# The samples' coefficients of a gated DeltaNet layer, computed beside the prompt's last recurrence, in a pool of their own

## The chip, the cores and the metric

One core of a Trainium2 chip runs the kernel, once per measurement. The metric is the time of one execution in device microseconds (us). Matrix products run on TensorE (PE in the profile; its weight loads are PEld), elementwise work on VectorE (DVE), ScalarE (ACT) and GpSimd (POOL). Every transfer between the chip's main memory and SBUF is issued on SyncE's queue (SP) and carried by 16 DMA engines.

## The reference

The reference is one inference step of a two-layer decoder trunk (model width 1024): a prompt of 1024 tokens, and eight samples of four tokens each that continue from stored caches and states. Layer 0 is sliding-window attention, layer 1 is gated DeltaNet with 16 value heads of width 128 and 8 key heads. Only layer 1 matters here. For each head it carries a state S (128 x 128):

```
S_t = e^{g_t} S_{t-1} + k_t u_t^T
u_t = beta_t (v_t - (e^{g_t} S_{t-1})^T k_t),    o_t = S_t^T q_t / sqrt(dk)
```

For the prompt this is done in chunks along the sequence, starting from zero. For a sample it is done for four tokens, starting from a stored state: 8 samples x 16 heads x 64 KB = 8.4 MB of states are read, and as much is written back as new states. The four steps are not run one by one over the states. With the products of the *old* state with all k and q, the four u and o follow from small coefficients between the four tokens, and the new state is the old one times a decay, plus the sum of k u^T. The output o is normalized, multiplied with a gate, and projected back to width 1024 (w_out, 2048 x 1024); the result is added to the residual, and a final norm gives y.

## The kernel before, in words

The kernel is one program for one core. Its last fifth, where the change lies, consists of an output projection with several smaller jobs woven into it.

**The order of the instructions** is settled when the program is built. Each engine runs its instructions in the order in which the builder recorded them (class `Core`, line 96, keeps modelled free times of the engines; line 89 is the line that all recorded instructions carry in the profile). A job is a Python generator. `weave` (line 483) puts it into a list, sorted by its rank in the table `K` (line 239); `stages` (line 494) is called between matmuls and lets each job advance whose next condition holds in the model: `ready` (operands written), `idle` (engine free), `soon`, `bank` (a PSUM bank of that name is free), `over` (the named jobs have ended). DMA issues on SP are placed by the surrounding scheduler. So the order of the engines reflects modelled times; on the chip an engine that meets an instruction whose operands are late waits, with everything behind it.

**The output projection** (`out_block`, line 2253) runs 18 blocks: 8 of 128 prompt rows and one of the 32 sample rows, first with weight rows 0 to 1023 (part 0), then with rows 1024 to 2047 (part 1). The block of the samples is number 8, and the last but one again in part 1. A prompt block takes 48 matmuls of 128x512 (three products of high and low halves, 8 row tiles, 2 column halves), a sample block 32, together 832. Each block needs two tiles `of` of gated rows (256 KB each, `prepare`, line 2136), a residual tile `xt` (512 KB, `rows_of`, line 2169), and stores 512 KB (`x2d` in part 0, the output y in part 1; `finish`, line 2183). At the samples' block the program opens larger buffers for the states (`wide`, line 2618), and `prepare` for it waits for the job "core" (line 2141).

**The jobs beside it**, in the order in which they depend on each other:

- "chain", "output", "gating" (lines 1935 to 2050): the prompt's last recurrence, eight chunks, each a sequence of TensorE, VectorE and ScalarE steps. It runs during the first blocks of the projection, which then uses the PSUM banks "pj" only.
- "states" (`states_times`, line 2312): reads all 8.4 MB of old states in pieces of 256 KB (four buffers) and multiplies them with the samples' k and q; the products end in `kqs`.
- "core" (line 2365): starts when the recurrence is over. Its **first half** (lines 2388 to 2469) needs no states: it loads the samples' q and k (`qk2`), v (`vs`), the decays (`gH`) and beta (`bH`) from a scratch tensor in main memory, transposes k to the update operand `K96` and q, k, v to a layout with one row per head and sample (`VH`, `QK0`, `QK1`), and computes norms, decays and the coefficients between the four tokens (`cK`, `cQ`, through the work tile `prd`). Its **second half** (from line 2470) waits for "states", transposes their products (`KQT`, `KQ`), computes the four u in place in `VH`, transposes them to the second update operand `U96` (line 2515), tells the job "new" to begin (`updates`, line 2516), and computes the samples' outputs into `gsT`.
- "load" (`second_half`, line 2547): loads and splits the second half of w_out (`whB`, `wlB`).
- "new" (`new_states`, line 2562): the stream of the new states. A piece of four heads (256 KB, pool `su`, three buffers, tile `S1`, shown as `S` in the profile) or, once `wide` is open, of eight heads (512 KB) is loaded; per two heads there is one matmul of `kb` (K96 masked for one sample) with `U96` into a bank of "mi" (two banks), and VectorE adds it to the decayed state; the piece is stored to `out_new_s_s`.

The tiles of "core" lie in a pool `sl` on the right side of SBUF, opened after the recurrence's pools are closed (lines 2368 to 2374); `K96`, `U96` and `gsT` lie on the left in `sp2`, then `kqs`, then the pool `sg` of "states".

Of the kernel before, what the change touches and what calls it, by code (L numbers as in the profile page):

```python
# [5 lines left out]
F32 = mybir.dt.float32  # L6
# [8 lines left out]
P = 128  # L15
# [5 lines left out]
DS = 4  # L21
# [7 lines left out]
HV = 16  # L29
# [188 lines left out]
def body(tc, I, O, cst_ap, dbg=None):  # L218
# [17 lines left out]
    ZB, VB, SB = 1, 3, 4  # L236
    SP = (2, 20)
    AM = (4, 8)
    K = dict(split=3, add=3, attend=12, turning=14, modulate=31, cached=9, wo=7, turn=0, ahead=6, taps=4, gating=5, decay=2, samples=28, load=5, mod=9, shape=9, decays=8, prepare=1, gather=11, finish=54, states=21, core=4, new=9)
    KR = [{'chain': 8, 'output': 9, 'solve': 5, 'invert': 21, 'blocks': 10, 'decayed': 0}, {'chain': 0, 'output': 3, 'solve': 12, 'invert': 10, 'blocks': 35, 'decayed': 35}, {'chain': 33, 'output': 2, 'solve': 22, 'invert': 19, 'blocks': 33, 'decayed': 34}, {'chain': 22, 'output': 12, 'solve': 3, 'invert': 4, 'blocks': 30, 'decayed': 17}, {'chain': 14, 'output': 0, 'solve': 1, 'invert': 17, 'blocks': 31, 'decayed': 57}, {'chain': 3, 'output': 13, 'solve': 6, 'invert': 20, 'blocks': 55, 'decayed': 29}, {'chain': 8, 'output': 1, 'solve': 11, 'invert': 20, 'blocks': 73, 'decayed': 34}, {'chain': 10, 'output': 8, 'solve': 4, 'invert': 28, 'blocks': 40, 'decayed': 44}]  # L240
    TB = (3, 6)
    SW = (1, 16)
# [240 lines left out]
    def weave(gen, name, hq=None):  # L483

        rank = KR[hq][name] if hq is not None else K[name]
        i = 0
        while i < len(jobs) and jobs[i][3] <= rank:
            i += 1
        jobs.insert(i, [lambda: True, gen, name, rank])

    def over(*names):
        return lambda: not any(e[2] in names for e in jobs)
# [25 lines left out]
    def ready(*ts):  # L518
        return lambda: plain() or nc.ready(ts) <= nc.free["tensor"]

    def soon(*ts):
        return lambda: plain() or nc.ready(ts) <= nc.free["tensor"] + AH
# [10 lines left out]
    def bank(tag):  # L533

        q = held.setdefault(tag, [])
        yield lambda: len(q) < banks[tag] or q[-banks[tag]] is None
        t = psb(tag)
        q.append(t.tensor.name)
        yield lambda: plain() or nc.after(nc.used, t, "tensor") <= nc.free["tensor"]
        return t  # L540

    def give(tag, t):
        q = held[tag]
        q[q.index(t.tensor.name)] = None
# [1058 lines left out]
    if True:  # L1603
# [694 lines left out]
        def flat(t_):  # L2298
            return t_.rearrange("p t d -> p (t d)")
# [2 lines left out]
        sp2 = es.enter_context(tc.tile_pool(name="sp2", bufs=1, side="left"))  # L2302

        K96 = sp2.tile([96, HQ * P], F32R, name="K96")
        U96 = sp2.tile([96, HV * P], F32R, name="U96")
        gsT = sp2.tile([P, HV, TS], F32, name="gsT")
        kq_guard = tc.tile_pool(name="kq", bufs=1, side="left")
        kqs = kq_guard.__enter__().tile([P, 2, 512], F32, name="kqs")
        sg_guard = tc.tile_pool(name="sg", bufs=1, side="left")
        sg = Watched(nc, sg_guard.__enter__())  # L2310

        def states_times():
            zq = sg.tile([P, DB, HQ, 32], F32, name="zq")
            qk = sg.tile([P, 4, P], F32, tag="S0", name="qk", bufs=SB).rearrange(
                "p a (c t) -> p (a c) t", t=TS).rearrange("p (i h) t -> p h i t", i=2)
            nc.sync.dma_start(qk.rearrange("p h i t -> p i h t"), smd[0:2 * HQ].rearrange("(i h) p t -> p i h t", i=2))
            us_ = [(g * 4 + b, hd, jj) for g in range(2) for hd in range(2) for b in range(4) for jj in range(2)]
            sts = []

            def fetch():  # L2320
                if len(sts) < len(us_):
                    b, hd, jj = us_[len(sts)]
                    st = sg.tile([P, 4, P], F32, tag="S0", name="S0", bufs=SB)
                    nc.sync.dma_start(st, S0[b][:, 8 * hd + 4 * jj:8 * hd + 4 * jj + 4])
                    sts.append(st)

            for b in range(DB):
                yield idle("gpsimd")
                nc.gpsimd.memset(zq[:, b], 0.0)
            for b in range(DB):  # L2330
                c0 = 8 * (b % 4)
                yield idle("vector", qk)
                nc.vector.tensor_copy(zq[:, b, :, c0:c0 + 8].rearrange("p h (i t) -> p h i t", i=2),
                                      qk[:, :, :, b * DS:(b + 1) * DS])
            for _ in range(SB):
                fetch()
            for u in range(0, len(us_), 2):
                b, hd, _ = us_[u]
                if u % 16 == 0:
                    pk = yield from bank("lg")  # L2340
                yield lambda: pos[0] >= SW[0] + SW[1] * (u + 1) / 10
                yield ready(sts[u], sts[u + 1], zq)
                for j in range(4):
                    nc.tensor.matmul(pk[32 * j:32 * j + 32, hd * 256:(hd + 1) * 256], zq[:, b, 4 * hd + j, :],
                                     sts[u + j // 2][:, 2 * (j % 2):2 * (j % 2) + 2, :].rearrange("p h d -> p (h d)"),
                                     start=(b % 4 == 0), stop=(b % 4 == 3), skip_group_check=True)
                fetch()
                fetch()
                if u % 16 == 14:
                    yield soon(pk)  # L2350
                    nc.scalar.copy(kqs[:, b // 4, :], pk)
                    give("lg", pk)
# [9 lines left out]

    updates, fng, gate_s, sl_guard, su_guard, wo2_guard = [], None, None, None, None, None

    def core():
        nonlocal sm, out_banks, sl_guard
        yield over("chain", "output", "gating")
        g_guard.__exit__(None, None, None)
        sm_guard.__exit__(None, None, None)
        gk_guard.__exit__(None, None, None)  # L2370
        sm = Watched(nc, sm_first, 2)
        out_banks = ("pj", "pj", "tr", "ob")
        sl_guard = tc.tile_pool(name="sl", bufs=1, side="right")
        sl = Watched(nc, sl_guard.__enter__(), since=nc.free["tensor"] + SL)

        def t2(nm, dt=F32):
            return sl.tile([P, DS, P], dt, tag="t2", name=nm, bufs=4)

        def turned(dst, srcs, parts=P):

            yield ready(*srcs)
            pt = yield from bank("lg")
            for q, src in enumerate(srcs):
                nc.tensor.transpose(pt[0:parts, q * P:(q + 1) * P], src, ident)
            yield soon(pt)
            dst(pt)
            give("lg", pt)

        qk = flat(t2("qk2")).rearrange("p (i h t) -> p i h t", i=2, h=HQ)
        nc.sync.dma_start(qk.rearrange("p i h t -> p (i h) t"), smd[0:2 * HQ].rearrange("n p t -> p n t"))  # L2390
        vs = t2("vs")
# [23 lines left out]
                nc.vector.tensor_copy(qv[:, t], src[:, t].unsqueeze(2).to_broadcast([P, HQ, 2, DB]))  # L2415
            QKH.append((yield from by_head(f"QK{i}", [qd[:, t, :] for t in range(DS)])))
        QH, KH = QKH

        def s4(nm, n=DS):
            return sl.tile([P, n], F32, name=nm)  # L2420

        yield idle("vector", gH)
        gcH = s4("gcH")
# [27 lines left out]
        for t in range(DS):  # L2451
            n = t + 1
            dc = s4(f"dc{t}")
            yield idle("vector")
            nc.vector.tensor_tensor(dc[:, 0:n], gcH[:, t:t + 1].to_broadcast([P, n]), gcH[:, 0:n], ALU.subtract)
            nc.scalar.activation(dc[:, 0:n], dc[:, 0:n], AF.Exp)
            yield idle("vector", dc)
            nc.vector.tensor_tensor(dc[:, 0:n], dc[:, 0:n], rkH[:, 0:n], ALU.mult)
            for dst, src in ((cQ, QH), (cK, KH)):
                m = n if dst is cQ else t  # L2460
                if m == 0:
                    continue
                yield idle("vector")
                nc.vector.tensor_tensor(pr_[:, 0:m], KH[:, 0:m], src[:, t:t + 1, :].to_broadcast([P, m, P]), ALU.mult)
                yield idle("vector")
                nc.vector.tensor_reduce(dst[:, t, 0:m], pr_[:, 0:m], AX.X, ALU.add)
                nc.vector.tensor_tensor(dst[:, t, 0:m], dst[:, t, 0:m], dc[:, 0:m], ALU.mult)
            if t > 0:
                nc.vector.tensor_scalar(cK[:, t, 0:t], cK[:, t, 0:t], rkH[:, t:t + 1], -1.0, ALU.mult, ALU.mult)
        yield over("states")  # L2470
        KQT = sl.tile([P, HV * DB, 2, DS], F32, name="KQT")
        kqv = KQT.rearrange("p (a j r g b) i t -> p g a r j (b i t)", a=2, j=4, r=2, g=2)
# [133 lines left out]
            nc.sync.dma_start(S1[b][:, h0:h0 + n], st)  # L2606

    weave(states_times(), "states")
    weave(core(), "core")
    weave(second_half(), "load")  # L2610
    weave(new_states(), "new")
# [9 lines left out]
    su_guard.__exit__(None, None, None)  # L2621
    sl_guard.__exit__(None, None, None)
    wo2_guard.__exit__(None, None, None)
    kq_guard.__exit__(None, None, None)
    ps_guard.__exit__(None, None, None)
    es.close()
# [30 lines left out]
```

## Time and profile before

| what | value |
|---|---|
| median of three runs | 1781.42 us (1780.93 to 1783.7) |
| execution that was profiled | 1771.52 us |
| span of its trace | 1769.7 us |
| granted TensorE clock, mean over the span | 0.984 |
| TensorE busy | 1671.2 us (94%) |
| last projection matmul of the trace begins | 1757.38 us |
| first and last store of a new state | issued at 1637.84 and 1754.43 us |

The profile is of one execution. Its page gives the busy time of each engine, and answers to questions about its trace give busy times by stretch, the waits by engine, and the instructions in order of time with the idle time of the engine before each and what ended it. Names stand for tiles ("ps_mi" is a PSUM tile of the banks "mi"). Overlapping matmuls each show their own latency; the distance between their starts is what they cost.

### The profile page before, as it was taken

Reading aid. Unit: us, or ns where it says so; the run is one execution under the profiler, and the core shown is the slowest. Engines: PE = TensorE matmul, PEld = TensorE weight load, DVE = VectorE, ACT = ScalarE, POOL = GpSimd, SP = SyncE. Lnnn points to the kernel's source line nnn. Section 1 sums busy time; section 2 is a strip of 40 time slices with the busy share of each in tenths; the row PEclk is TensorE's granted clock in tenths of the full one; section 3 lists DMA queues with packets and bytes.
Section 4 is the critical chain, followed back from the end, with each engine's and each line's share of the span. In section 5 each row is a group of like instructions: output and inputs, shape, how many; then the busy total and the mean of one; then the engine's idle time right before and its main releaser. Section 6 shows DMA issues by size and latency. Waiting matters only on the chain. (4 is left out here: it accounts for less than half of the span.)

```text
span 1769.7 us, 32005 instructions
## 1 busy us (share of the span) xinstructions
PE 1671.2 (94%) x10665; PEld 1452.1 (82%) x10665; DVE 1217.1 (69%) x3536; ACT 860.4 (49%) x2513; POOL 625.8 (35%) x1264
## 2 busy tenths in 40 slices
PE   6999999998998698989999999999999998998897
PEld 5978888877776698879989999899999997766685
DVE  4526676554565577886888779788787795458687
ACT  4625565453334446446554564654655664433332
POOL 2501111122112146343453545454445455323322
PEclk9999999999999799999999999999999999999999
DMA  9442122233332231231322323224133127774886
GB/s 325 134 119 59 50 63 54 67 105 101 102 113 89 69 86 47 72 101 35 112 69 58 103 57 105 64 61 119 42 100 84 46 75 205 212 208 129 256 255 184
DMA packets 282582, 191.78 MB, mean 108 GB/s; under 512 B 99369, under 2 KB 254889, under 8 KB 282386
## 3 DMA queue, kind: packets, MB, share of 16 engines
q1 hardware_dynamic: 282418, 189.75, 36.9%
q8 instruction: 84, 1.38, 0.3%
q14 instruction: 80, 0.66, 0.1%
HBM read 144.68 MB, written 47.04 MB: 108 GB/s over the span
## 5 line engine op out<-in xcount | busy, mean ns | idle before, releaser
L89 PE MATMUL ps_pj<-h2hi,wh 128*128 128x384 f32 (+1 forms) x1140 | 387.3, 340 | 2.6 <-ACT wh L89 2.6
L89 PE MATMUL ps_pj<-h2lo,wh 128*128 128x384 f32 (+1 forms) x1140 | 389.1, 341 | 0.0
L89 PE MATMUL ps_pj<-h2hi,wl 128*128 128x384 f32 (+1 forms) x1140 | 384.6, 337 | 1.2 <-POOL wl L89 1.2
L89 POOL TENSOR_TENSOR wl<-wr,wh 128x512 fp32r<-128x512 f32 x123 | 165.4, 1347 | 540.5 <-ACT wh L89 482.1
L89 PEld LDWEIGHTS ps_pj<-h2hi,wh 128*128 128x128 f32 x1140 | 217.2, 190 | 6.5 <-ACT wh L89 3.1
L89 PEld LDWEIGHTS ps_pj<-h2hi,wl 128*128 128x128 f32 x1140 | 217.2, 191 | 5.8 <-POOL wl L89 2.6
L89 PEld LDWEIGHTS ps_pj<-h2lo,wh 128*128 128x128 f32 x1140 | 217.0, 190 | 4.4
L89 POOL TENSOR_TENSOR xt<-xt,y 128x512 f32<-128x512 f32 (+1 forms) x48 | 65.2, 1361 | 196.3 <-DVE y L89 175.3
L89 DVE SCALAR_TENSOR_TENSOR vT<-XR,cT,vT 128x384 f32<-128x384 f32 (+1 forms) x144 | 92.6, 649 | 41.8 <-ACT vT L89 39.7
L89 PE MATMUL ps_pj<-hlo,wh 128*128 128x384 f32 (+1 forms) x360 | 119.3, 332 | 0.0
L89 PE MATMUL ps_pj<-hhi,wh 128*128 128x384 f32 (+1 forms) x360 | 118.6, 330 | 0.0
L89 PE MATMUL ps_pj<-hhi,wl 128*128 128x384 f32 (+1 forms) x360 | 117.9, 328 | 0.0
L89 DVE TENSOR_TENSOR tmp<-X 64x31 f32<-64x31 f32 (+15 forms) x248 | 96.1, 387 | 8.0 <-POOL X L89 4.3
L89 DVE TENSOR_TENSOR X<-X,tmp 64x31 f32<-64x31 f32 (+15 forms) x248 | 92.8, 374 | 8.5
L89 ACT CAST wh<-wr 128x512 fp32r<-128x512 f32 x123 | 75.4, 615 | 17.0 <-PE ps_pj L89 14.5
L89 PEld LDWEIGHTS ps_pj<-hlo,wh 128*128 128x128 f32 x360 | 67.7, 188 | 13.6 <-issue 13.5
L89 POOL TENSOR_TENSOR Xd<-Xc,cst 32x128 f32<-32x128 f32 x128 | 68.5, 535 | 14.8 <-DMA Xc<-Xdd 7.5
L89 PEld LDWEIGHTS ps_pj<-hhi,wh 128*128 128x128 f32 x360 | 67.6, 188 | 5.9 <-issue 4.2
L89 PEld LDWEIGHTS ps_pj<-hhi,wl 128*128 128x128 f32 x360 | 67.7, 188 | 3.3 <-issue 3.3
L89 ACT ACTIVATE qe<-ps_mi,Eg 128x128 f32<-128x128 f32 x112 | 35.0, 363 | 67.6 <-PE ps_mi L89 67.6
L89 ACT ACTIVATE prob<-prob,nm 128x256 f32<-128x256 f32 (+1 forms) x128 | 62.3, 489 | 11.3 <-DVE nm L89 11.1
L89 ACT COPY XR<-ps_pj 128x384 f32<-128x384 f32 (+1 forms) x96 | 43.1, 449 | 47.1 <-PE ps_pj L89 46.4
(564 smaller groups left out, 4281.2 us busy)
## 6 DMA issues: line engine op xcount, KB each, us to landing
wr<-in_gdn_w_in SPq DMA_DIRECT2D x96, 256.0 KB
S<-in_state_gdn_s SPq DMA_DIRECT2D x40, 256.0 KB
xt<-in_x_prompt SPq DMA_DIRECT2D x16, 512.0 KB
wm<-in_w_mod SPq DMA_DIRECT2D x16, 512.0 KB
wr<-in_swa_w_in SPq DMA_DIRECT2D x64, 128.0 KB
wm<-in_w_mod SPq DMA_DIRECT2D x32, 256.0 KB
wmod<-in_w_mod SPq DMA_DIRECT2D x32, 256.0 KB
DP<-gcr SPq DMA_DIRECT2D x64, 128.0 KB
```

What stands on the lines that cost most here:

```text
L89: inst = fn(*args, **kwargs)
```

## The change

The first half of "core" becomes a job of its own, "early", with rank 22 (behind "states" with 21). It no longer waits for the recurrence. Its tiles come from a new pool `sla` on the left side, opened before `sg`, so that it doesn't need the memory which the recurrence's pools hold; the tiles of the four steps that rotate under the tag "t2" come from it too. `U96` moves from `sp2` to the pool `sl` on the right. "core" waits for the recurrence and for "early", takes over its results and goes on with its second half. All other ranks stay. The number of instructions on TensorE is the same, and so is the arithmetic.

```diff
-    K = dict(..., states=21, core=4, new=9)
+    K = dict(..., states=21, early=22, core=4, new=9)
...
-        U96 = sp2.tile([96, HV * P], F32R, name="U96")
+        U96 = None
...
+        sla_guard = tc.tile_pool(name="sla", bufs=1, side="left")
+        sla = Watched(nc, sla_guard.__enter__(), since=nc.free["tensor"])
         sg_guard = tc.tile_pool(name="sg", bufs=1, side="left")
...
+    def t2(nm, dt=F32):
+        return sla.tile([P, DS, P], dt, tag="t2", name=nm, bufs=4)
...
+    early_ = {}
+
+    def core_early():
+
+        sl = sla
         qk = flat(t2("qk2")).rearrange("p (i h t) -> p i h t", i=2, h=HQ)
         nc.sync.dma_start(qk.rearrange("p i h t -> p (i h) t"), smd[0:2 * HQ].rearrange("n p t -> p n t"))
         vs = t2("vs")
...
                 nc.vector.tensor_scalar(cK[:, t, 0:t], cK[:, t, 0:t], rkH[:, t:t + 1], -1.0, ALU.mult, ALU.mult)
+        early_.update(VH=VH, gcH=gcH, bH=bH, at=at_, kd=kdH, eg=egH, rq=rqH, cK=cK, cQ=cQ, pr=pr_)
+
+    def core():
+        nonlocal sm, out_banks, sl_guard, U96
+        yield over("chain", "output", "gating")
+        yield over("early")
+        VH, gcH, bH, at_, kdH, egH, rqH, cK, cQ, pr_ = (early_[n] for n in ("VH", "gcH", "bH", "at", "kd", "eg", "rq", "cK", "cQ", "pr"))
+        g_guard.__exit__(None, None, None)
...
+        U96 = sl.tile([96, HV * P], F32R, name="U96")
         yield over("states")
...
     weave(states_times(), "states")
+    weave(core_early(), "early")
     weave(core(), "core")
```

More of the change, by code (lines that the diff above doesn't have):

```diff
@@ L238, in body @@
     AM = (4, 8)
-    K = dict(split=3, add=3, attend=12, turning=14, modulate=31, cached=9, wo=7, turn=0, ahead=6, taps=4, gating=5, decay=2, samples=28, load=5, mod=9, shape=9, decays=8, prepare=1, gather=11, finish=54, states=21, core=4, new=9)
+    K = dict(split=3, add=3, attend=12, turning=14, modulate=31, cached=9, wo=7, turn=0, ahead=6, taps=4, gating=5, decay=2, samples=28, load=5, mod=9, shape=9, decays=8, prepare=1, gather=11, finish=54, states=21, early=22, core=4, new=9)
     KR = [{'chain': 8, 'output': 9, 'solve': 5, 'invert': 21, 'blocks': 10, 'decayed': 0}, {'chain': 0, 'output': 3, 'solve': 12, 'invert': 10, 'blocks': 35, 'decayed': 35}, {'chain': 33, 'output': 2, 'solve': 22, 'invert': 19, 'blocks': 33, 'decayed': 34}, {'chain': 22, 'output': 12, 'solve': 3, 'invert': 4, 'blocks': 30, 'decayed': 17}, {'chain': 14, 'output': 0, 'solve': 1, 'invert': 17, 'blocks': 31, 'decayed': 57}, {'chain': 3, 'output': 13, 'solve': 6, 'invert': 20, 'blocks': 55, 'decayed': 29}, {'chain': 8, 'output': 1, 'solve': 11, 'invert': 20, 'blocks': 73, 'decayed': 34}, {'chain': 10, 'output': 8, 'solve': 4, 'invert': 28, 'blocks': 40, 'decayed': 44}]
@@ L2363, in body, with s4, turned @@
     updates, fng, gate_s, sl_guard, su_guard, wo2_guard = [], None, None, None, None, None
[L2365 to L2387, printed above, removed]
+    def t2(nm, dt=F32):
+        return sla.tile([P, DS, P], dt, tag="t2", name=nm, bufs=4)
+    def s4(nm, n=DS):
+        return sla.tile([P, n], F32, name=nm)
+    def turned(dst, srcs, parts=P):
+        yield ready(*srcs)
+        pt = yield from bank("lg")
+        for q, src in enumerate(srcs):
+            nc.tensor.transpose(pt[0:parts, q * P:(q + 1) * P], src, ident)
+        yield soon(pt)
+        dst(pt)
+        give("lg", pt)
+    early_ = {}
+    def core_early():
+        sl = sla
         qk = flat(t2("qk2")).rearrange("p (i h t) -> p i h t", i=2, h=HQ)
@@ L2417, in core @@
         QH, KH = QKH
-        def s4(nm, n=DS):
-            return sl.tile([P, n], F32, name=nm)
         yield idle("vector", gH)
@@ L2469, in core @@
                 nc.vector.tensor_scalar(cK[:, t, 0:t], cK[:, t, 0:t], rkH[:, t:t + 1], -1.0, ALU.mult, ALU.mult)
+        early_.update(VH=VH, gcH=gcH, bH=bH, at=at_, kd=kdH, eg=egH, rq=rqH, cK=cK, cQ=cQ, pr=pr_)
[5 more added lines that the diff above has]
+        g_guard.__exit__(None, None, None)
+        sm_guard.__exit__(None, None, None)
+        gk_guard.__exit__(None, None, None)
+        sm = Watched(nc, sm_first, 2)
+        out_banks = ("pj", "pj", "tr", "ob")
+        sl_guard = tc.tile_pool(name="sl", bufs=1, side="right")
+        sl = Watched(nc, sl_guard.__enter__(), since=nc.free["tensor"] + SL)
+        U96 = sl.tile([96, HV * P], F32R, name="U96")
         yield over("states")
@@ L2623, in body @@
     wo2_guard.__exit__(None, None, None)
+    sla_guard.__exit__(None, None, None)
     kq_guard.__exit__(None, None, None)
```

## The prediction

> **What bounds the kernel now.** I read the page's head, then the busy times of five engines by stretch from the end of the last projection on, then what TensorE (PE) waited for there. In a stretch's row the last three numbers are the granted TensorE clock, the DMA engines' share and GB/s.
>
> ```profile
> span 1769.7 us, 32005 instructions
> PE 1671.2 (94%) x10665; PEld 1452.1 (82%) x10665; DVE 1217.1 (69%) x3536; ACT 860.4 (49%) x2513; POOL 625.8 (35%) x1264
> ```
>
> ```profile
> 1494.00:1560.00 66.00, 63.05 (x367) 45.94 (x367) 27.10 (x82) 24.39 (x81) 20.98 (x58) 0.97 0.78 225
> 1560.00:1637.00 77.00, 67.56 (x323) 49.64 (x322) 56.72 (x148) 27.58 (x54) 25.55 (x18) 1.00 0.51 157
> 1637.00:1660.00 23.00, 17.63 (x79) 12.32 (x78) 15.83 (x33) 8.58 (x18) 9.81 (x8) 0.99 0.82 255
> 1660.00:1740.00 80.00, 79.97 (x361) 64.95 (x361) 59.47 (x204) 24.41 (x58) 24.68 (x19) 0.98 0.86 256
> ```
>
> ```profile
> PE ps_mi L89 <- DVE S L89: 4.8, 1, 4.8
> PE ps_mi L89 <- ACT uo L89: 3.1, 2, 2.2
> PE ps_lg L89 <- DVE KQT L89: 3.1, 1, 3.1
> PE ps_mi L89 <- ACT kb L89: 2.1, 2, 1.3
> PE ps_tr L89 <- POOL olo L89: 1.8, 1, 1.8
> ...
> PE ps_lg L89 <- DVE qd L89: 0.9, 1, 0.9
> PE ps_lg L89 <- DMA qk<-smd: 0.8, 1, 0.8
> ```
>
> TensorE sets the end. From 1660 to 1740 us it is busy 79.97 of 80 us. In the 77 us before the sample states start to stream it is idle 9.4, and in the 23 us in which they start, 5.4. It runs its instructions in an order that was written down when the program was built, so a wait is lost for good. The change adds no arithmetic and removes none: it can win idle time only, and it loses each wait that it makes. That caps the gain: the two idle stretches hold 14.8 us.
>
> Next, what TensorE needs for one instruction of the output projection (128x512) and for one state update (ps_mi<-U,kb), and how the stream of the states began.
>
> ```profile
> 1583.16 0.39 PE L89 MATMUL ps_pj<-h2hi,ohi 128*128 128x512 f32 x1
> ...
> 1589.73 0.39 PE L89 MATMUL ps_pj<-h2lo,ohi 128*128 128x512 f32 x1
> ```
>
> ```profile
> 1752.64 0.28 PE L89 MATMUL ps_mi<-U,kb 96*128 96x256 f32 x1
> 1752.75 0.39 PE L89 MATMUL ps_tr<-h2hi,ohi 128*128 128x512 f32 x1
> ```
>
> ```profile
> 1634.07 0.28 PE L89 MATMUL ps_mi<-U,kb 96*128 96x256 f32 x1
> ...
> 1659.82 0.55 PE L89 MATMUL ps_mi<-U,kb 96*128 96x256 f32 x1 [4.85 <-DVE S L89]
> ...
> 1665.47 0.28 PE L89 MATMUL ps_mi<-U,kb 96*128 96x256 f32 x1
> ```
>
> The first pair is 29 steps apart: 6.57 / 29 = 0.2265 us per projection instruction; there are 832 of them, and I use their running number as a place in the program. The second pair gives 0.11 us per update instruction. The third shows the first eight pieces of the states (256 KB each): from the last update of piece 1 (number 372) to that of piece 8 (number 466) lie 94 projection instructions and 14 updates, 94 x 0.2265 + 14 x 0.11 = 22.8 us of work, and 31.4 us passed. **8.6 us were lost while the states came in small pieces.** Afterwards, with pieces of 512 KB, nothing was lost. This is the stretch that the change makes longer.
>
> **The change part by part.** *What moves.* The built programs' order (no times in it) shows that the block from the loads of the samples' q, k, v to the coefficients cK now stands beside the last recurrence. In the trace of before it ran here:
>
> ```profile
> 1572.69 0.85 DVE L89 COPY qd<-qk 128x128 f32<-128x128 f32 x4
> ...
> 1602.23 0.23 DVE L89 TENSOR_SCALAR cK<-cK,rkq 128x3 f32<-128x3 f32 x1
> ```
>
> The last input of the updates, U, is written at number 324 in the program of before and at number 224 in the new one: 100 x 0.2265 = 22.7 us earlier. The first piece leaves at number 287 instead of 372. From number 462 on the buffers of 512 KB are open in the new program (466 before), since that hangs on block 8 of the projection. So **18 pieces of 256 KB and 7 of 512 KB** take the place of 8 and 12, and the states end at number 658 instead of 811.
>
> *What it wins.* The waits for qd, qk, KQT and olo (0.9 + 0.8 + 3.1 + 1.8 = 6.6 us) come from VectorE working through the moved block while TensorE needs copies that stand behind it; with VectorE free there, I let 5.5 us go and keep 1.1 for what is late next (TensorE still needs KQT through a copy on ScalarE and one on VectorE). The second wait for kb (1.3 us of the 2.1) sits at number 765, where no updates are left: it goes as well. Gain: 6.8 us. The 4.8 us for S I do not count as won, because its kind returns below.
>
> *What the small pieces cost.* Two bounds apply to 18 of them. First the work: from number 287 to 462 lie 175 x 0.2265 + 34 x 0.11 = 43.4 us of TensorE. Second the traffic. Counting the built program's DMA issues from behind the first small store to the last: 17 stores and 15 loads of 256 KB, 2 loads of 512 KB, 5 tiles of gated rows (of), 9 moves of 512 KB of the residual (xt, x2d; two of them are the samples' 128 KB), 3 weight pieces and the final gain: 16.5 MB. TensorE at full speed would ask for 16.5 / 43.4 us = 380 GB/s. The same count from small store 1 to 8 in the program of before gives 7.86 MB, and these are their issues:
>
> ```profile
> 1637.84 1.38 SPq L89 DMA_DIRECT2D out_new_s_s<-S  x2
> ...
> 1666.43 0.38 SPq L89 DMA_DIRECT2D out_new_s_s<-S  x1
> ```
>
> 7.86 MB in 28.6 us is 275 GB/s by the stores, in 31.4 us 250 by the updates, where the work alone (22.8 us) asked for 345; the 80 us after it ran at 256 with a share of 0.86. I take 265 GB/s: 16.5 MB then need 62.3 us, and 62.3 - 43.4 = 18.9 us are lost instead of 8.6, so **10.3 us more**. The wait passes from a piece's load to VectorE, which updates in order, from there to the two PSUM banks of the updates, and so to TensorE. With 250 GB/s it is 14.0 more, with 275 8.0. The ends: the fastest and slowest 4 us with a DMA share of 1.09,
>
> ```profile
> 1552.00:1556.00 4.00, 3.64 (x17) 2.67 (x15) 1.17 (x2) 0.00 (x0) 1.28 (x1) 1.00 1.09 238
> 1564.00:1568.00 4.00, 3.87 (x26) 2.03 (x23) 0.00 (x0) 0.00 (x0) 0.16 (x1) 1.00 1.09 361
> ```
>
> give 361 GB/s (45.7 us, 6.3 less than before) and 238 (69.3 us, 17.3 more). The Trainium skill, "DMA: Bandwidth & Descriptors", Specifications, gives a ceiling of about 358 GB/s of HBM per core; by it (an estimate) the 16.5 MB take 46 us, next to nothing is lost, and the change wins. That is the first rival. The row at 361 agrees with that figure as a peak of 4 us; no longer stretch here comes near it.
>
> *The large pieces.* From the last small store to the last large one the new program moves 12.3 MB in 196 x 0.2265 + 28 x 0.11 = 47.5 us, 259 GB/s; 256 was carried without loss. Cost 0, at most 2.
>
> *The start.* Four loads come up from here to the front of the SP queue, behind the projection's first residual tiles:
>
> ```profile
> 1551.36 0.37 SPq L89 DMA_DIRECT2D qk<-smd  x1
> 1551.78 3.15 SPq L89 DMA_DIRECT2D vs<-smd  x1
> 1554.98 1.13 SPq L89 DMA_DIRECT2D gH<-gbr  x1
> 1556.15 0.43 SPq L89 DMA_DIRECT2D bH<-gbr  x1
> ```
>
> That is 5.1 us of SP. Queued behind: two weight pieces (ScalarE splits them for the projection), two tiles of gated rows, the first states. TensorE needs the second half of the gated rows from number 24 on, 24 x 0.2265 = 5.4 us into the projection; the cover is nearly whole. In TensorE's own order the transposes of k stand right after the gate rows, so TensorE waits if they have not landed, and VectorE's step of the recurrence stands behind their copies. Between 0 and 4 us; I take 1. TensorE waits at that place before, too, for the recurrence's uo, so part of it is not new.
>
> *Beside the recurrence.* 20 transposes, their copies, at most the 29.8 us of VectorE between the two rows above, and a table load on ScalarE fall into 1494 to 1560 us, where VectorE is busy 27.1 of 66 and ScalarE 24.4. TensorE has the projection to fill with, as its 63.05 of 66 show. Between 0 and 3; I take 1. What U's move to the pool on the right costs: nothing, its memory is free before U is written.
>
> **Sum.** -5.5 - 1.3 + 10.3 + 0 + 1 + 1 = **+5.5 us** on the span of 1769.7 (1775.2). The execution with the profile took 1771.52 us, the median of the runs shown is 1781.42, 0.56% more; I carry the difference over: 1781.4 + 5.5 = **1786.9 us**. Differences under 0.2% (3.6 us) a measurement of this kernel can hardly tell from none.
>
> One thing can add to a long wait:
>
> ```profile
> 1656.00:1660.00 4.00, 0.18 (x1) 0.21 (x2) 1.28 (x4) 1.43 (x3) 1.26 (x1) 0.96 0.72 229
> 1660.00:1664.00 4.00, 4.00 (x13) 3.24 (x14) 1.78 (x6) 0.61 (x2) 1.27 (x1) 0.61 0.93 263
> ```
>
> After the wait of 4.85 us the granted clock is 0.61 for 4 us: some 1.5 us more. It is within the 31.4 us above, and so in the rate. The Trainium skill, "TensorE: Matmul & The Clock Gate", The HAM clock gate, says the same: half the clock after an idle window of about 3.4 us. By it many short waits cost only themselves.
>
> **The rivals.**
> *A: the DMA engines have room, and the change wins.* Place: the small pieces. It decides at the rate at which the loss there is 8.6 + 4.8 = 13.4 us: 16.5 MB in 56.8 us, 290 GB/s. At 330 (50.0 us, 6.6 lost) the sum is -5.5 - 1.3 - 2.0 + 2 = -6.8: 1774.6 us. For it: the peak of 361, and the DMA share of 0.82 in the first 23 us. Against: three buffers of 256 KB must be loaded, updated, stored and loaded again, and every stretch over 20 us lies at 225 to 256.
> *B: both cancel,* at 280 to 300 GB/s: 1781.4.
> *C: the start decides.* If the samples' k or the weights behind them land 4 us late and the recurrence is held as well, 4 + 3 instead of 2 are added: 1791.9. For it: the transpose of k that stands right behind the gate rows in TensorE's order. Against: the load goes out in the place of one that landed in time.
> *D: the block does not run earlier* since some wait of it stands with the old end: 1781.4. The built order speaks against it (224 for 324).
>
> **How the numbers follow.** Forecast (small pieces at 240 to 280 GB/s): 0.46. A 0.28, B 0.15, C 0.09, D 0.02. Slower by over 0.2%: 0.46 + 0.09 = 0.55; within: 0.17; faster: 0.28. The forecast's own range is 1783 to 1794. The bounds of the unknown costs reach from -5.5 - 1.3 - 6.3 = -13.1 (1768) to -6.8 + 17.3 + 2 + 4 + 3 = +19.5 (1801). Leaving out a tenth at each end: **1770 to 1797**, which takes in A and C.
>
> **What would show it.** Right: the first store of a sample state about 23 us earlier (85 x 0.2265 = 19.3, and 3.5 of waits gone), no wait for KQT or qd, an idle TensorE of some 19 us between the first and the last small store at about 265 GB/s with waits for S and kb, none after. Wrong: TensorE full in that stretch at over 290 GB/s (A), or idle before 1510 us (C).

## The result, and the profile after the change

| | kernel before | changed kernel |
|---|---|---|
| median of 20 runs each | 1780.9 us (1774.97 to 1790.59) | 1785.44 us (1780.55 to 1791.58) |
| execution with the profile | 1771.52 us | 1784.83 us |

**The change makes the kernel slower: ratio 1.003, 95% interval 1.0017 to 1.0043.** The medians are 4.5 us apart. In a second comparison (run "again", below) the medians are 7.5 us apart and the ratio was 1.0041, 1.0026 to 1.0056. The forecast was +5.5 us. The two profiled executions are 13.3 us apart, more than that: the one of before is 9.4 us under the median of the 20 runs (it is not one of them, and it is quicker than the quickest, 1774.97), the one of after 0.6 under. So sizes are taken from the ratios first, and from traces where several of them agree.

The page of the changed kernel begins:

```profile
span 1783.0 us, 32028 instructions
PE 1678.2 (94%) x10665; PEld 1453.6 (82%) x10665; DVE 1215.4 (68%) x3536; ACT 861.4 (48%) x2513; POOL 629.5 (35%) x1264
```

On TensorE the two programs have the same order up to the transposes of k that stand in front of the projection. I set the clock to zero at a TensorE instruction ahead of it (the eight ps_lg<-UZ,M of 128x96, at 1485.15 us before and 1489.14 after: 4.0 of the 13.3 us have passed by then) and cut the rest at the projection's instructions number 40, 159, 287 and 462 (counted from 0; the last is number 831). Busy times by stretch, the kernel before and then the changed one; first the stretch and its length, then PE, PEld, DVE, ACT and POOL, at the end granted clock, DMA share and GB/s:

```profile
1485.15:1517.09 31.94, 28.10 (x146) 20.12 (x147) 15.79 (x51) 13.73 (x41) 10.59 (x31) 0.89 0.82 238
1517.09:1565.02 47.93, 46.34 (x278) 32.52 (x274) 15.81 (x41) 15.03 (x47) 17.20 (x39) 1.00 0.82 233
1565.02:1607.84 42.82, 37.06 (x175) 27.50 (x173) 34.21 (x88) 16.59 (x34) 14.91 (x10) 1.00 0.56 177
1607.84:1664.55 56.71, 48.47 (x217) 36.24 (x216) 40.68 (x99) 19.67 (x38) 19.44 (x14) 0.97 0.58 176
1664.55:1757.38 92.83, 91.54 (x420) 73.59 (x418) 71.02 (x246) 30.10 (x71) 25.98 (x20) 1.00 0.81 244
```

```profile
1489.14:1530.79 41.65, 32.02 (x162) 22.43 (x163) 19.03 (x59) 16.78 (x47) 10.68 (x24) 0.88 0.75 200
1530.79:1581.51 50.72, 49.04 (x293) 34.01 (x290) 31.88 (x99) 17.44 (x56) 17.75 (x45) 0.97 0.75 220
1581.51:1622.59 41.08, 37.51 (x172) 28.73 (x170) 30.93 (x71) 18.28 (x34) 12.43 (x9) 0.96 0.52 158
1622.59:1681.77 59.18, 48.89 (x212) 36.29 (x211) 36.49 (x90) 16.47 (x34) 21.43 (x16) 0.97 0.86 255
1681.77:1772.35 90.58, 89.08 (x399) 71.04 (x398) 61.23 (x206) 26.22 (x63) 29.11 (x21) 1.00 0.64 202
```

The reader is to see two things. The fourth row is the small pieces: the DMA share went from 0.58 to 0.86 and the stretch grew by 2.5 us only. The first row is the start, and it grew by **9.7 us**; there the forecast had 1. What TensorE waited for in the changed kernel from 1480 us on, the largest first (total, times, longest):

```profile
PE ps_mi L89 <- DVE S L89: 8.4, 8, 2.7
PE ps_lg L89 <- DMA S<-in_state_gdn_s: 4.8, 1, 4.8
PE ps_lg L89 <- DVE oH L89: 3.5, 1, 3.5
PE ps_mi L89 <- ACT kb L89: 3.2, 2, 1.7
PE ps_lg L89 <- DMA qk<-smd: 2.1, 1, 2.1
PE ps_mi L89 <- ACT uo L89: 2.0, 1, 2.0
PE ps_tr L89 <- ACT vo L89: 1.7, 1, 1.7
```

The waits for qd, KQT and POOL's olo are gone. The wait for qk grew from 0.8 to 2.1 and moved from the middle to the start; the largest one for the *old* states grew from 0.7 to 4.8 and moved to the start too. New are one for vo, and eight shorter ones for S where there was one of 4.85. The wait for oH grew from 1.43 to 3.5.

**The start, followed back.** In order of time, rows of TensorE, ScalarE, GpSimd and SP from the changed kernel:

```profile
1501.34 0.60 PE L89 MATMUL ps_lg<-cst,qk 128*32 128x128 f32 x4 [2.08 <-DMA qk<-smd]
1501.97 1.16 ACT L89 CAST K<-ps_lg 32x512 fp32r<-32x512 f32 x2 [2.81 <-PE ps_lg L89]
...
1503.43 1.16 ACT L89 CAST K<-ps_lg 32x512 fp32r<-32x512 f32 x2
...
1510.16 0.60 ACT L89 CAST h2hi<-wr 128x512 fp32r<-128x512 f32 x1
...
1514.84 0.20 POOL L89 TENSOR_TENSOR fo<-rst,rsw 128x4 f32<-128x4 f32 x1
1514.99 1.29 POOL L89 TENSOR_TENSOR h2lo<-wr,h2hi 128x512 fp32r<-128x512 f32 x1
...
1516.31 0.33 SPq L89 DMA_DIRECT2D wr<-in_gdn_w_out  x1
1517.20 2.57 SPq L89 DMA_DIRECT2D S<-in_state_gdn_s  x4
...
1523.01 1.91 PE L89 MATMUL ps_lg<-S,zq 128*32 128x256 f32 x8 [4.85 <-DMA S<-in_state_gdn_s]
```

Read it from below. TensorE waits 4.85 us for two pieces of old states. SP issued them at 1517.20, because it could issue the weight load wr, which stands ahead of them, only at 1516.31. That load needs the buffer which GpSimd reads in h2lo, and h2lo ended at 1516.28; SP's longest wait from 1480 to 1530 us, 3.8 us, is put down to h2lo. GpSimd had it behind a chain of the recurrence's rsqrt (up to fo), since ScalarE's last two splits h2hi stand behind the copies of k to K96 now, and those behind TensorE's transposes, which waited for qk. In the kernel before, GpSimd did that h2lo ahead of the chain:

```profile
1498.41 1.27 POOL L89 TENSOR_TENSOR olo<-of,ohi 128x512 fp32r<-128x512 f32 x1 [7.81 <-ACT ohi L89]
1499.64 1.27 POOL L89 TENSOR_TENSOR h2lo<-wr,h2hi 128x512 fp32r<-128x512 f32 x1
1504.31 0.20 POOL L89 TENSOR_TENSOR rst<-rsw 128x4 f32<-128x4 f32 x1 [3.40 <-DVE rsw L89]
```

After such waits the granted clock (the third number from the end) is low for some us more. At the start it is low from 1496 to 1508 us, behind the wait of 2.00 us for uo (which ends at 1494.03) and around the one for qk; then behind those for the old states, for vo and for oH:

```profile
1496.00:1500.00 4.00, 3.26 (x7) 1.52 (x6) 1.39 (x4) 1.70 (x3) 0.00 (x0) 0.63 0.99 275
...
1504.00:1508.00 4.00, 4.00 (x19) 3.38 (x19) 2.02 (x7) 2.07 (x6) 0.00 (x0) 0.77 0.98 294
...
1524.00:1528.00 4.00, 4.00 (x20) 2.77 (x16) 0.60 (x2) 0.12 (x1) 0.00 (x0) 0.71 0.61 164
```

```profile
1564.00:1568.00 4.00, 4.00 (x17) 2.22 (x18) 3.52 (x14) 0.20 (x1) 0.00 (x0) 0.59 0.93 254
1618.00:1622.00 4.00, 2.91 (x9) 2.52 (x10) 3.87 (x8) 1.46 (x2) 0.65 (x1) 0.57 0.57 180
```

So two theories stand against each other. **P**, the prediction's: the early stream of small pieces costs the time. **S**, the prediction's rival C, later sharpened to **Q**: the start costs it, by what stands in front of what.

### The profile page after: what moved, and what is told of

It reads as the page before. It is cut to its first block, busy times and chain, and to the rows that moved or that the text cites. A ratio compares the mean times of both kernels' runs of the same rounds, so it can differ in the third digit from the quotient of the medians.

```text
span 1783.0 us, 32028 instructions
## 1 busy us (share of the span) xinstructions
PE 1678.2 (94%) x10665; PEld 1453.6 (82%) x10665; DVE 1215.4 (68%) x3536; ACT 861.4 (48%) x2513; POOL 629.5 (35%) x1264
## 5 line engine op out<-in xcount | busy, mean ns | idle before, releaser
L89 DVE SCALAR_TENSOR_TENSOR vT<-XR,cT,vT 128x384 f32<-128x384 f32 (+1 forms) x144 | 92.8, 651 | 40.5 <-ACT vT L89 38.5
L89 DVE TENSOR_TENSOR X<-X,tmp 64x31 f32<-64x31 f32 (+15 forms) x248 | 92.8, 374 | 8.5
```

What stands on the lines that cost most here:

```text
L89: inst = fn(*args, **kwargs)
```

## The experiments

Twelve runs follow; the first of them is the changed kernel once more. Ratios are to the kernel before on the same chip; the four lengths are read from one trace each, between the instructions named above (us). Most sizes below are differences of two ratios, often from different chips. By their intervals such a difference is uncertain by about 0.002, which is 3 to 4 us: a gain of 4 us is only just clear of none.

| kernel | ratio, 95% interval | zero to 40 | 40 to 287 | 287 to 462 | 462 to the last |
|---|---|---|---|---|---|
| before | 1 | 31.9 | 90.8 | 56.7 | 92.8 |
| changed | 1.0030 [1.0017, 1.0043] | 41.7 | 91.8 | 59.2 | 90.6 |
| again | 1.0041 [1.0026, 1.0056] | 39.3 | 92.0 | 59.2 | 89.9 |
| hold | 1.0004 [0.9990, 1.0018] | 41.8 | 91.8 | 47.4 | 94.5 |
| loads | 1.0050 [1.0033, 1.0067] | 34.3 | 85.1 | 66.7 | 91.9 |
| pm | 1.0041 [1.0027, 1.0056] | 38.5 | 92.1 | 60.4 | 90.8 |
| gate3 | 1.0019 [1.0004, 1.0035] | 35.9 | 92.6 | 58.4 | 90.7 |
| gate3hold | 0.9980 [0.9964, 0.9995] | 35.4 | 92.8 | 46.4 | 93.7 |
| sb6 | 0.9983 [0.9967, 1.0000] | 32.9 | 91.0 | 59.5 | 90.7 |
| bufs6 | 1.0006 [0.9995, 1.0017] | 41.6 | 91.7 | 52.5 | 92.7 |
| bsb6 | 0.9970 [0.9954, 0.9987] | 33.0 | 91.1 | 53.0 | 97.1 |
| sb6hold | 0.9957 [0.9941, 0.9974] | 33.4 | 90.3 | 49.1 | 94.3 |
| sb6bufs6 | 0.9962 [0.9946, 0.9978] | 32.1 | 90.5 | 54.2 | 89.9 |
| best | 0.9948 [0.9930, 0.9967] | 27.7 | 92.2 | 48.7 | 94.1 |

### again: the changed kernel a second time

> The changed kernel unchanged, for a second profile. Theory P (the prediction's: the small pieces of the state stream cost 10.3 us, the start 1): ratio to the kernel before 1.003, and again some 19 us lost between the first and last small store. Theory S (the start: the loads of the samples' q, k and v stand in front of the first gated rows, weights and states, and TensorE waits there): ratio 1.003, and again about 8 us more than before from the gate rows to projection instruction 40, with a wait for qk near 2 us and one for the first states near 5 us. If the wait for the states is missing here, it was an accident of one execution, and S loses that part.

Measured: 1782.86 against 1775.33 us, and the same waits: 2.43 us for qk, 4.00 for the old states. In all five traces with the changed start (changed, again, hold, pm, bufs6) the first column is 38.5 to 41.8. The wait is no accident of one execution.

### hold: the stream starts where it started before

```diff
-        yield lambda: updates
+        yield lambda: updates and pos[0] >= 124
```

> The coefficients and U are computed as early as in the changed kernel (U at number 224), but the stream of the new states may begin only at number 372, as before: 8 small pieces and 12 large ones again. Theory P: the 10.3 us of the small pieces go, the 1.3 of the second kb wait come back: 5.5 - 10.3 + 1.3 = -3.5 us against before, ratio 0.998. Theory S: the start stays, and the stream's place changes next to nothing (in the two profiles 2.5 us more up to number 462, 2.3 less behind it): ratio 1.002 to 1.004, like the changed kernel.

Measured: 1776.22 us, 6.6 less than "again", no longer to be told from before. The stretch from 287 to 462 shrinks from 59.2 to 47.4:

```profile
1622.45:1669.84 47.39, 44.62 (x193) 34.53 (x191) 25.64 (x52) 12.70 (x26) 21.11 (x15) 0.96 0.69 216
```

Eighteen of the updates go with it (16 against 34 begin in this stretch, 2.0 us at 0.11) and are done later, in the last column. **The early stream costs 6.6 us**; P has its mechanism, S's "next to nothing" falls. But P expected hold to beat the kernel before by 3.5, and it doesn't: as much as the early coefficients win is lost at the start.

### loads: only the four loads early

```diff
+        yield over("chain", "output", "gating")
         for h4 in range(2):
             yield from turned(lambda pt: halves(K96, ...
@@ second_half
         yield over("states")
+        yield lambda: sl_guard is not None
```

> Only the four loads (qk2, vs, gH, bH) go to the front of the SP queue; transposes, copies and coefficients wait for the end of the recurrence as before (U at number 334, before 324; the stream begins at 384, before 372). Theory P: the start costs 1 us, the block runs where it ran: ratio 1.000 to 1.001. Theory S: the loads delay weights, gated rows and first states behind them by some 8 us of SP, and TensorE waits for states: 3 to 6 us, ratio 1.002 to 1.004; no wait for qk, since nothing needs it early.

Measured: 1.005, slower than either theory had it. The first column is 2.4 us over before (a wait of 3.55 for uo, 2.17 before). From 40 to 287 it is 5.7 us shorter than before, from 287 to 462 10.0 us longer, with waits for olo, oH, the samples' rows and kb of 1.8 to 4.6 us each: U came at number 334, and the second half of the weights was held too (memory demands it). As a test of the loads alone it is not clean; that part stays open. One thing it does show, against S: TensorE waits for old states only 0.2 us at a time at the start, so the four loads in front of the states did not make the wait of 4 to 5 us.

### pm: the same loads in pieces of 2 KB

```diff
-    smd = dr.tile([48, P, TS], F32, name="smd")
+    smd = dr.tile([P, 48, TS], F32, name="smd")
@@ and the two stores to it, smd[:, n], and the four loads, such as
-        smd[2 * HQ:2 * HQ + HV].rearrange("n p t -> p n t")
+        smd[:, 2 * HQ:2 * HQ + HV]
```

> The changed kernel with the scratch tensor of the samples' q, k, v and z laid out partition-major in main memory, so that the four loads from it move 2 KB per partition in one piece instead of 16 pieces of 128 B; sizes, queue order and the order on all engines stay. Theory P: at most 1 us better than the changed kernel (ratio to before 1.0025). Theory S: the issue of vs (4.4 us), ong (2.8) and gH (1.3) on SP shrinks to about 0.4 each, weights and states come some 6 us earlier, the waits for qk and the states go: 4 to 7 us better than the changed kernel, ratio to before 0.999 to 1.001.

Measured: 1.0041, as the changed kernel. On SP the issues shrank; first the changed kernel, then pm:

```profile
1490.02 2.78 SPq L89 DMA_DIRECT2D ong<-in_gdn_o_norm_g  x1
...
1495.30 4.36 SPq L89 DMA_DIRECT2D vs<-smd  x1
```

```profile
1487.14 0.47 SPq L89 DMA_DIRECT2D ong<-in_gdn_o_norm_g  x1
...
1490.10 0.78 SPq L89 DMA_DIRECT2D vs<-smd  x1
```

The first old states were issued some 4 us earlier, and still TensorE waited 3.93 us for the fifth and sixth piece: these stand behind the weight load which waits for GpSimd. It also waited 1.85 us ahead of the transposes of k. So the small pieces of the four loads are not what delays the states (their bytes stayed the same, and no run changes those). The Trainium skill, "Perfetto Trace Analysis", What "DMA-bound" means, counts a solid issuing track among the bounds of a kernel and names large descriptors as the remedy. The trace agrees on the remedy for the track (4.36 to 0.78 us); it was no bound of this kernel by itself.

### gate3: the splits of the weights ahead of the copies of k

```diff
+        yield lambda: pos[0] >= 3
         for h4 in range(2):
             yield from turned(lambda pt: halves(K96, ...
```

> The changed kernel, but the transposes of k wait for projection instruction 9; the four loads, U at number 224 and the stream at 287 stay. By the built order, the last two splits of weights (h2hi on ScalarE, h2lo on GpSimd) stand ahead of the copies of k and of the recurrence's rsqrt again, as before the change. Theory Q (order, not bytes: in the changed kernel a weight load on SP waits for its buffer until GpSimd's h2lo, which stands behind those copies and the rsqrt; the states' fifth and sixth piece stand behind that load on SP, and TensorE waits 4 to 5 us for them, then runs 4 us at a clock near 0.6): the wait for qk (2.1 to 2.6 us) and the wait for the states (4 to 5 us) go, 6 to 8 us better than the changed kernel, ratio to before 0.999 to 1.001. Theory P (the stream's small pieces are all of the loss, the start costs 1 us): ratio 1.003 to 1.004, like the changed kernel.

Measured: 1.0019, 3.9 us better than "again", at the edge of what two ratios can tell; the trace is clearer. The waits for qk and for the fifth and sixth piece are gone; one of 1.3 for later states came. But another wait took part of the gain. ScalarE meets the split of a weight that has not landed, since its load stands behind the four new ones on SP, and uo, which the recurrence needs, stands behind that split. ScalarE's row in gate3, then what TensorE waited for:

```profile
1507.56 0.62 ACT L89 CAST h2hi<-wr 128x512 fp32r<-128x512 f32 x1 [6.64 <-DMA wr<-in_gdn_w_out]
1508.08 0.37 ACT L89 COPY uo<-ps_ob 128x256 f32<-128x256 f32 x1
```

```profile
PE ps_mi L89 <- ACT uo L89: 6.3, 2, 4.6
```

Q holds for the chain; its 6 to 8 us were too many.

### gate3hold: both

> As gate3, and the stream of the new states held to number 372 as in hold. If the two costs are separate and add up (start 6 to 8 us, stream 6.6 us, by 1.0041 against 1.0004): 6 to 8 us better than hold, ratio to before 0.996 to 0.997, faster than both kernels. If the states that come in time only make TensorE wait later (for oH, vo or the two lg banks), it stays near hold: 0.999 to 1.000.

Measured: 0.9980, 4.3 us better than hold (1.0004 to 0.9980), about what gate3 won without hold. As far as these sizes can tell, the start and the stream are separate costs and add up. The size is below the one written down, as in gate3.

### sb6: two more buffers for the old states, and its control bsb6

```diff
-    ZB, VB, SB = 1, 3, 4
+    ZB, VB, SB = 1, 3, 6
```

> The changed kernel with six buffers for the old states instead of four: by the built order two more state pieces are issued on SP ahead of the weight load that waits. Nothing else moves at the start: the copies of k still stand ahead of the splits. Theory Q: the wait for the states (4 to 5 us and the slow clock behind it) goes, the wait for qk (2 us) stays: 3 to 6 us better than the changed kernel, ratio 1.001 to 1.002. If the wait is one of transfer rate and not of order, it only moves to a later piece: ratio 1.004.

Measured: 0.9983, 10.3 us better than "again", more than expected. The first column falls from 39 to 42 down to 32.9, and in sb6 only these are left at the start:

```profile
PE ps_mi L89 <- ACT uo L89: 2.1, 1, 2.1
PE ps_lg L89 <- DMA qk<-smd: 1.6, 1, 1.6
```

The same edit in the kernel before:

> Control: the kernel before the change, with six buffers for the old states instead of four, and nothing else (U at number 307 instead of 324). Its waits for old states were 0.7 us each. Theory Q (the six buffers undo a wait that the change made): ratio 0.998 to 1.001. If six buffers help any version by themselves: ratio 0.994 to 0.997, and what sb6 won says nothing of the change.

Measured: 0.9970. Six buffers win 5.3 us in the kernel before as well, where they also move U from number 324 to 307. So only some 5 of sb6's 10.3 us are the change's, and by the intervals that 5 is uncertain by as much. What the traces do show is that the wait for old states at the start, 4 to 5 us in the changed kernel, is gone in sb6. Why the kernel before wins, its trace doesn't tell: there is one profile of it, of a quick execution, and bsb6's profile is no shorter (in the table 274.2 against 272.2 from zero to the last). This stays open.

### bufs6: three more buffers for the new states

```diff
-                st = su.tile([P, 4, P], F32, tag="S1", name="S1", bufs=3)
+                st = su.tile([P, 4, P], F32, tag="S1", name="S1", bufs=6)
```

> The changed kernel with six buffers of 256 KB for the new states instead of three; the order on TensorE stays. Theory R (rate: 16.5 MB between the first and the last small store need 60 us at 257 to 263 GB/s): the stretch stays at 59 to 60 us, ratio 1.003 to 1.0045. Theory B (three buffers: a piece can't be loaded before another was stored): the waits for S go, up to 7 us better than the changed kernel, ratio near 1.000, and over 290 GB/s in the stretch.

Measured: 1.0006, 6.2 us better than the 1.0041 of "again". By stretch, 287 to 462:

```profile
1621.57:1674.10 52.53, 46.28 (x211) 35.34 (x210) 38.41 (x90) 16.48 (x34) 20.18 (x15) 1.00 0.91 276
```

The same work and the same pieces took 52.5 instead of 59.2 us, at 276 instead of 255 GB/s. Waits from 1621 us on, in bufs6:

```profile
PE ps_mi L89 <- ACT kb L89: 6.3, 3, 2.8
PE ps_mi L89 <- DVE S L89: 2.0, 4, 1.2
```

S went from 8.4 to 2.0; kb on ScalarE grew from 3.2 to 6.3. **Three buffers, not the transfers' rate, set the 255 GB/s** (B against R). At over 290 GB/s B was wrong: 276 were reached. The 358 GB/s of the Trainium skill, "DMA: Bandwidth & Descriptors", Specifications, are not reached in any of these stretches.

### sb6hold, sb6bufs6 and best: the cures together

"best" is gate3, sb6, hold and pm in one.

> The changed kernel with six buffers for the old states and the stream of the new ones held to number 372. If the two costs add up (sb6 took the changed kernel from 1.0041 to 0.9983, hold from 1.0041 to 1.0004): ratio 0.994 to 0.996, faster than both kernels. If the held stream pushes the waits behind number 372: 0.997 to 0.999.

> Six buffers for the old states and six for the new ones, the stream not held. Theory B (the three buffers limit the small pieces; bufs6 took 1.0041 to 1.0006): ratio 0.994 to 0.996. Theory R (the transfers limit them as soon as the start is quicker): 0.997 to 0.999, at most 277 GB/s in the stretch of the small pieces as in bufs6.

> gate3, sb6, hold and the scratch tensor partition-major (2 KB per partition in one piece), together. In gate3 ScalarE waited 6.64 us for a weight load behind the four loads, and TensorE 4.58 us for uo behind it; in pm the weights behind the four loads were issued some 4 us earlier. If that wait shrinks to the 2.2 us of before: ratio 0.992 to 0.995. If the four loads cost by their bytes and not by their pieces: like gate3hold with the states in time, 0.996 to 0.998.

Measured: 0.9957, 0.9962 and 0.9948; the last is 1766.33 against 1775.26 us, faster than both kernels. Most of that is not the change's: bsb6, the kernel before with the same six buffers for old states, took 1770.61 us on the same chip, 3.5, 3.2 and 4.3 us more than the three. In the first two the gains add up nearly, by holding the stream back or by giving it buffers. sb6bufs6 against sb6 (54.2 and 59.5 us from 287 to 462) repeats bufs6. In best the wait of 4.6 us for uo behind the weights, as gate3 had it, is down to 1.1 us, below the 2.2 that was written down for it: with the small pieces of the four loads gone, ScalarE meets the weights in time. The first column (27.7) overstates the gain: some 15 matmuls stood ahead of number 40 in sb6hold and stand behind it in best, and of the 5.7 us between the two 1.9 come back in the second column. Waits of TensorE in best:

```profile
PE ps_mi L89 <- ACT kb L89: 4.9, 3, 2.7
PE ps_lg L89 <- DVE oH L89: 3.5, 1, 3.5
PE ps_mi L89 <- ACT uo L89: 2.8, 2, 1.6
PE ps_pj L89 <- DVE y L89: 1.4, 1, 1.4
```

The interval of best overlaps those of the two others, so what pm and gate3 add to sb6hold is not shown by the ratios, and no run has best without pm.

## Why the prediction was right, step by step

The sign and the size were right: +5.5 forecast, +4.5 and +7.5 by the medians of the two comparisons. That the sum came out so well is luck in part: one of its terms was wrong, and another erred in the opposite direction.

- **The block moves.** Right. The first store of a new state was issued at 1623.42 us, 134.3 after zero, before 152.7: 18.4 us earlier, forecast some 23. It is 4.6 short, with a start that is longer than forecast.
- **The win, -5.5, and +1 beside the recurrence.** Right in size. hold and before differ in both respects and not in the stream's place: from number 40 to the last instruction hold takes 233.7 us, before 240.3. Of these 6.6 us, 1.5 are four groups of transposes (some 0.37 each) that now stand ahead of number 40; about 5 remain, forecast 4.5. It rests on one trace each, but others agree: from number 40 to the last, gate3hold, sb6hold and best take 232.9, 233.7 and 234.9 us, bsb6 241.2. The waits named for it are gone (KQT, qd, olo), but what is late next was larger than the 1.1 kept: oH 3.5 instead of 1.43, vo 1.7.
- **The small pieces, +10.3, and the second kb wait, -1.3.** Right mechanism, too large: 9.0 together, 6.6 by hold against again. The stretch itself was well forecast: 15.8 us lost in 287 to 462 (59.18 less the 43.4 of work), forecast 18.9; 255 GB/s, forecast 265. Two things were wrong in the comparison. The kernel before lost more in the same numbers than the 8.6 us counted from number 372 on, since its waits for oH, kb and olo lie between 287 and 372. And the rate was taken as what the transfers can do, while bufs6 shows that it followed from three buffers.
- **The large pieces, 0.** From 462 to 658 the changed kernel took 50.6 us for 47.5 of work, 1.5 of it a wait for kb: 3 instead of at most 2. The early stream is not the reason, since hold takes 50.7 us in the same numbers.
- **The start, +1 (0 to 4): the step that failed.** What is left of the 7.5 us between again and before when the win (5) and the stream (6.6, hold against again on the same chip) are taken out is 7.5 + 5 - 6.6 = 5.9 us, an estimate from medians and traces together (with the 4.5 us of the first comparison it would be 2.9); gate3 takes back 3.9 of it, sb6 some 5 beyond its control, each uncertain by about as much; in the traces the first column is 9.7 and 7.4 us longer (changed, again), of which 1.5 are the moved transposes. The prediction said that "the load goes out in the place of one that landed in time" and let one us go. It counted SP's 5.1 us and looked for direct waits. It did not follow the order of ScalarE and GpSimd: copies of k ahead of two weight splits, one of these behind the rsqrt on GpSimd, its buffer ahead of a weight load on SP, that load ahead of the states.
- **The rivals.** C named this place, with 4 + 3 us and a chance of 0.09. Its price was about right, its mechanism only in part (k came 2.1 us late; the larger wait was for the old states), its total not, since the small pieces cost less. A needed 290 GB/s; with three buffers 255, with six 276 were reached. Against A the prediction said that every stretch over 20 us lies at 225 to 256 GB/s; its own row from 1560 to 1637 us shows 157, which does not change the forecast. D fell.
- **The clock.** As forecast, the granted clock falls to 0.57 to 0.71 for some 4 us behind the waits of 3.5 and 4.85 us, and such a wait costs that much more. That short waits cost only themselves did not hold (last section).

## What to carry to other kernels

When a job is moved forward, follow each instruction that it issues on *every* in-order engine, and ask which older instruction now stands behind it and who waits for that one: four copies of 0.6 us on ScalarE, whose input came late, made TensorE wait 4.85 us by way of GpSimd and the queue of loads, as the chain in the trace has it; with the splits ahead of the copies (gate3) that wait was gone. A throughput seen in a trace is a limit of the transfers only if more buffers don't raise it; here three more buffers did, from 255 to 276 GB/s, and undid most of a loss that looked like bandwidth. And what early results start can cost more than they win: the stream held to its old place, with the rest moved, was 6.6 us faster.

## What was not expected of the hardware

- A load in pieces of 128 B, right behind another such load, held SP's queue for 4.36 us, and a 0.5 KB load behind such a one for 2.78; with 2 KB per partition in one piece, and the same bytes, 0.78 and 0.47. The kernel's time did not move by it alone (1.0041 both).
- A wait of 1.7 us (for vo) was enough for a granted clock of 0.59 over the next 4 us. The forecast had concluded from the Trainium skill, "TensorE: Matmul & The Clock Gate", The HAM clock gate, that short waits cost only themselves. The length alone does not decide: in the same trace the wait of 2.37 us for S that ends at 1636.39 us was followed by a clock of 1.00 (1636 to 1640), the one of 2.68 us that ends at 1644.58 by 0.60 (1646 to 1650). What decides is not shown.
- The profiled execution of the kernel before was 0.5% under the median of the 20 runs, more than the whole effect. The two single profiles would have put the change at 13 us.
